# Weight units stored as they stand on chip, tokens stored transposed, norm scales moved behind the projections: a streaming-encoder block on one Trainium2 core

## The chip, the cores and the metric

The kernel runs on one core of one Trainium2 chip. The core has a matrix engine (PE, with PEld for its weight loads), a vector engine (DVE), a scalar engine (ACT), a general engine (POOL) and a queue engine (SP) that issues most transfers; 16 DMA engines move data between the main memory and the on-chip memory. Matmuls write to banks of PSUM, a small memory of which each bank holds 128 x 512 float32 numbers. The metric is device time of one execution in microseconds (us), as the median over runs. The arrays that the kernel is given may be laid out in any way on the host, without arithmetic; that is not part of the time.

## What is computed

All numbers are float32; there are 2048 tokens of 1024 channels.

```python
def reference(x, norm_mix_g, w_in, f_bias, sg_ln_g, sg_w, sg_b, w_out, norm_ffn_g, w_up, w_conv, b_conv, w_down, norm_final_g):
    h = rms_norm(x, norm_mix_g)                  # x * rsqrt(mean(x*x) + eps) * g
    z = h @ w_in                                 # 1024 -> 512 u, 512 v, 512 q, 512 k, 512 values, 8 forget logits
    u, v = gelu(z[:, :512]), gelu(z[:, 512:1024])
    out_a = spatial_gating(u, v, sg_ln_g, sg_w, sg_b)   # u * (masked sg_w @ layernorm(v) + sg_b), blocks of 128 tokens
    c = cumsum(log_sigmoid(f_logit + f_bias))    # per head, over the tokens
    out_b = softmax(q @ k.T / 8 + c[t] - c[s], s <= t) @ values   # 8 heads of 64
    x = x + concat(out_a, out_b) @ w_out
    a = causal_conv3(rms_norm(x, norm_ffn_g) @ w_up, w_conv) + b_conv   # 1024 -> 2 x 2816
    x = x + (silu(a[:, :2816]) * a[:, 2816:]) @ w_down
    return rms_norm(x, norm_final_g)
```

## The kernel before

Each float32 matmul is made of three matmuls in a faster format: both operands are split into a high part and a low part (what the rounding of the high part leaves), and high x high, high x low and low x high are summed in one PSUM bank (`mm3`, L202). So every operand goes through a copy that rounds (on ACT or POOL) and a subtraction on DVE.

The work runs in stages. Stage A (`phase_a`) handles the tokens in two halves of 1024, each of two half-blocks of 512. It normalizes the tokens, turns them so that channels lie on the partitions, splits them, and projects them to keys, queries, values, the two gate inputs u and v, and the forget logits. In the first half the order is keys, queries, values, gates; in the second it is gates, values, queries after keys. From the gates of the first half on, the attention (`b_stream`) is woven in between: `tick` counts matmuls, and each time the count passes a rate (`RATES`) one more step of the attention is issued. Stage C (`c_half`) multiplies by `w_out`, stage D (`d_half`) by `w_up` for the first half; for the second half of the tokens `late_half` does both, and `down` multiplies by `w_down` for all. In the last two, seven products replace eight.

What the change touches, in the kernel before:

- **Weights.** `load_unit` (L151) loads a unit of 128 x 1024 numbers by one DMA on SP (`raw`), casts it to the high part on POOL (L149) and subtracts on DVE (L161). A narrow unit is 128 columns of `w_in` or `w_up` for all eight groups of 128 channels: each row of the matrix that it reads gives 512 B, so a unit is 1024 pieces of 512 B. A wide unit (values and gates, `w_out`) is two groups by 512 columns, 256 pieces of 2 KB. In `late_half`, `up_raw` (L1143) loads narrow units of `w_up` by itself.
- **Tokens.** `a_rows` (L347) loads rows of x (128 tokens x 1024), squares and sums them on ACT (L358), forms the scale on DVE and POOL (L361, L362, a power of -0.5), and in the first half multiplies the rows by it on DVE (L366). `a_norm` (L369) then turns each 128 x 128 piece by PE with an identity matrix (L182, four to a bank), and `split` copies the bank to the high part on ACT with the norm's weight g as a scale (L191) and forms the low part on DVE (L192). For the second half the rows are loaded a second time as [128 tokens, 4, 256 channels], scaled on POOL (L399), and turned in the same way, behind counts of matmuls (`defer`).
- **Small columns.** The per-channel vectors (norm weights, gate bias, convolution) are loaded as rows by seven DMAs (`columns`) and turned by two transposes (`columns_turn`, L266).
- **Gate weights.** `a_gate_w` loads `sg_w`, zeroes the masked part on POOL and turns eight matrices on PE.
- **Projections.** `channels` computes a block of 128 key or query channels by 512 tokens in a bank, copies the high part on ACT (L416), subtracts on DVE (L417) and writes both to memory by four DMAs. `token_major` does values and gates with tokens on the partitions.
- **Constants.** `a_consts` and `b_consts` (masks, a triangle, ones) are filled on POOL behind the first scales.

The order of the instructions on each engine is made by a planner, from priorities and modelled costs: the code gives data flow, priorities (`high_priority`), and a few forced orders (`issue_after`, which queues a block's instructions behind one instruction on the same engine). Rings of buffers have the sizes in `BUFS`; a load into a ring waits until the last reader of the old content is done. The banks `mm` are two.

Of the kernel before, what the change touches and what calls it, by code (L numbers as in the profile page):

```python
# [8 lines left out]
F32 = mybir.dt.float32  # L9
# [23 lines left out]
AHEAD_B, AHEAD_W = 100, 2000  # L33
LAG = 2
# [45 lines left out]
class Block:  # L80
# [70 lines left out]
    def load_unit(self, src, inner):  # L151
# [6 lines left out]
        self.raw_ins = self.dma(v(raw), src).ins  # L158
# [56 lines left out]
    def constants(self):  # L215
# [6 lines left out]
        self.colA = cp.tile([P, 112], F32, name="colA")  # L222
        self.colB = cp.tile([P, 88], F32, name="colB")
# [15 lines left out]
    def columns(self):  # L239

        nc, a = self.nc, self.a
        r0 = self.til(self.sp, [P, TB], F32, "st")[:112, :P]
        r1 = self.til(self.sp, [P, TB], F32, "st")[:88, :P]
        cv = a["w_conv"][0].rearrange("w (c p) -> w c p", p=P)
        self.dma(r0[0:8, :], a["norm_mix_g"][0].rearrange("(c p) -> c p", p=P))
        self.dma(r0[8:16, :], a["norm_ffn_g"][0].rearrange("(c p) -> c p", p=P))
        self.dma(r0[16:24, :], a["sg_b"][0])
        self.dma(r0[24:68, :], cv[0])
        self.dma(r0[68:112, :], cv[1])
        self.dma(r1[0:44, :], cv[2])  # L250
        self.dma(r1[44:88, :], a["b_conv"][0].rearrange("(c p) -> c p", p=P))
        self.rows_c = r0, r1
        self.g_mix = self.colA[:, 0:8]
        self.g_ffn = self.colA[:, 8:16]
        self.sgb = self.colA[:, 16:24]
        self.cw0 = self.colA[:, 24:68]
        self.cw1 = self.colA[:, 68:112]
        self.cw2 = self.colB[:, 0:44]
        self.cb = self.colB[:, 44:88]

    def columns_turn(self):
        nc = self.nc
        r0, r1 = self.rows_c
        for r, n, col in ((r0, 112, self.colA), (r1, 88, self.colB)):
            ps = self.til(self.ap, [P, TB], F32, "tp")
            nc.tensor.transpose(ps[:, :n], r, self.ident[:n, :n])  # L266
            nc.vector.tensor_copy(col, ps[:, :n])

        for t in (self.colA[:, 46:68], self.colA[:, 90:112], self.colB[:, 22:44], self.colB[:, 66:88]):
            nc.vector.tensor_scalar(t, t, 0.5, None, ALU.mult)  # L270


    def phase_a(self):
        tc = self.tc
        with ExitStack() as es:
# [9 lines left out]
            for c in range(2):  # L285
                with tc.issue_after(self.lo_ins[2 + 3 * c]):
                    self.first.append(self.a_unit("k", c))
# [1191 lines left out]
```

## Time and profile before

| | |
|---|---|
| median of 3 runs | 2469.13 us (2466.55 to 2471.33) |
| the profiled execution | 2466.4 us |
| its span, first to last instruction | 2464.6 us |
| busy: PE / DVE / ACT / POOL | 2420.7 / 1740.5 / 1341.4 / 332.0 us |
| moved by DMA | 396.33 MB, 161 GB/s on average |
| PE clock granted, mean | 0.999 of full speed |

The profile page gives busy times and a picture of the span; a trace behind it can be asked for groups of instructions by line, for single instructions in order of time (the timeline), for who waited for whom (the waits), for busy times in chosen stretches (the windows), for one tile's instructions, and for the chain of waits that ends with the last instruction. In such rows `tp<-ident,x` names the tile written and the tiles read, `x46` is a count, and what stands behind the last bar is the engine's idle time before these instructions with what it waited for. A PE row's duration is that of one matmul from entering to leaving; matmuls follow each other before that, so the spacing of their starts is the cost and not the duration.

### The profile page before, as it was taken

What the parts mean: (1) busy time and instruction counts of PE and PEld (TensorE: products, weight loads), DVE (VectorE), ACT (ScalarE), POOL (GpSimd) and SP (SyncE); (2) the same over time, 40 slices, a digit from 0 to 9 for tenths busy, and PEclk for the clock granted to TensorE, in tenths of its full rate; (3) what the DMA queues carried; (4) which work ended last, traced back from release to release, by engine and by line L of the source; (5) the groups of instructions that cost most, each with busy time, mean ns of one, the idle gap of its engine ahead of it and who ended that gap; (6) DMA issues with size and microseconds to landing.
All of it is one profiled execution on the core that took longest, in us unless ns stands there. A gap on an engine that the chain in (4) does not pass through costs nothing.

```text
span 2464.6 us, 32929 instructions
## 1 busy us (share of the span) xinstructions
PE 2420.7 (98%) x11082; PEld 1989.8 (81%) x11082; DVE 1740.5 (71%) x3060; ACT 1341.4 (54%) x2629; POOL 332.0 (13%) x335
## 2 busy tenths in 40 slices
PE   7999999999999999999999999999999999999998
PEld 5788878878878778788888878878888887888887
DVE  6237677565556777878878775488888887957775
ACT  4226676554355555767677673365555555444443
POOL 3214222010113311112111011100000000001000
PEclk9999999999999999999999999999999999999999
DMA  7863544767856544555555445412222329538633
GB/s 209 243 163 105 175 119 135 187 185 208 274 178 205 182 148 157 170 161 181 163 163 181 154 153 205 158 54 93 77 77 88 92 70 319 166 100 289 210 115 121
DMA packets 346244, 396.33 MB, mean 161 GB/s; under 512 B 52924, under 2 KB 222084, under 8 KB 344652
## 3 DMA queue, kind: packets, MB, share of 16 engines
q1 hardware_dynamic: 341036, 370.11, 48.8%
q0 software_dynamic: 5040, 24.12, 2.5%
q8 instruction: 88, 1.44, 0.3%
q14 instruction: 80, 0.66, 0.1%
HBM read 300.56 MB, written 93.72 MB: 160 GB/s over the span
## 4 chain that ended last, share of the span: by engine, by line
PE 88%; DMA 4%; DVE 3%; ACT 2%; issue 1%; POOL 1%; SPq 0%; POOLq 0%; DVEq 0%; ACTq 0%
PE D L1335 16%; PE mm L211 13%; PE mm L209 13%; PE mm L207 13%; PE A L1132 3%; PE A L1134 3%; PE A L1133 3%; PE o L774 2%; PE o L773 2%; PE s L786 2%; PE s L785 2%; PE s L725 2%; PE s L724 2%; PE B L1133 2%; PE B L1134 2%; PE B L1132 2%
## 5 line engine op out<-in xcount | busy, mean ns | idle before, releaser
L207 PE MATMUL mm<-thi,whi 128*128 128x512 f32 x960 | 377.4, 393 | 2.6 <-DVE vn L417 2.0
L209 PE MATMUL mm<-tlo,whi 128*128 128x512 f32 x960 | 377.5, 393 | 0.0
L211 PE MATMUL mm<-thi,wlo 128*128 128x512 f32 x960 | 376.4, 392 | 0.1
L207 PE MATMUL mm<-whi,thi 128*128 128x512 f32 x640 | 253.2, 396 | 1.1 <-DMA thi<-mixh 1.0
L211 PE MATMUL mm<-whi,tlo 128*128 128x512 f32 x640 | 251.1, 394 | 0.8 <-DMA tlo<-mixl 0.8
L209 PE MATMUL mm<-wlo,thi 128*128 128x512 f32 x640 | 250.8, 392 | 0.2 <-DVE wlo L161 0.2
L149 POOL TENSOR_SCALAR whi<-raw 128x1024 fp32r<-128x1024 f32 x108 | 126.5, 1172 | 908.4 <-PE mm L209 551.6
L733 ACT ACTIVATE s<-s,part 128x512 f32<-128x512 f32 (+3 forms) x257 | 150.8, 587 | 151.2 <-DVE part L728 85.4
L207 PEld LDWEIGHTS mm<-thi,whi 128*128 128x128 f32 x960 | 180.4, 188 | 41.8 <-DVE vn L417 2.3
L211 PEld LDWEIGHTS mm<-thi,wlo 128*128 128x128 f32 x960 | 180.5, 188 | 37.9 <-DVE wlo L161 0.6
L209 PEld LDWEIGHTS mm<-tlo,whi 128*128 128x128 f32 x960 | 180.5, 188 | 37.3
L797 DVE TENSOR_TENSOR pl<-e,ph 128x512 fp32r<-128x512 f32 (+2 forms) x212 | 136.7, 652 | 64.1 <-ACT ph L796 31.8
L161 DVE TENSOR_TENSOR wlo<-raw,whi 128x1024 fp32r<-128x1024 f32 x108 | 143.7, 1331 | 50.0 <-POOL whi L149 44.3
L791 ACT ACTIVATE e<-s 128x512 f32<-128x512 f32 (+2 forms) x227 | 116.1, 529 | 83.3 <-DVE s L789 41.6
L1335 PE MATMUL D<-wl,xh 128*128 128x512 f32 x368 | 141.5, 389 | 0.0
L1335 PE MATMUL D<-wh,xh 128*128 128x512 f32 x368 | 140.8, 389 | 0.2 <-DVE xo L1413 0.2
L207 PEld LDWEIGHTS mm<-whi,thi 128*128 128x128 f32 x640 | 120.6, 188 | 24.9 <-DMA thi<-mixh 1.4
L211 PEld LDWEIGHTS mm<-whi,tlo 128*128 128x128 f32 x640 | 120.3, 188 | 24.9 <-DMA tlo<-mixl 1.3
L209 PEld LDWEIGHTS mm<-wlo,thi 128*128 128x128 f32 x640 | 120.6, 188 | 23.2 <-DVE wlo L161 0.4
L1335 PE MATMUL D<-wh,xl 128*128 128x512 f32 x368 | 137.3, 389 | 0.0
L796 ACT ACTIVATE ph<-e 128x512 fp32r<-128x512 f32 (+2 forms) x212 | 117.2, 563 | 36.4 <-PE o L773 29.1
L728 DVE TENSOR_REDUCE part<-s 128x1 f32<-128x512 f32 x144 | 94.8, 683 | 28.3 <-PE s L725 27.6
(1885 smaller groups left out, 5786.3 us busy)
## 6 DMA issues: line engine op xcount, KB each, us to landing
raw<-in_w_up_dram SPq DMA_DIRECT2D x72, 512.0 KB
m<-kx SPq DMA_DIRECT2D x133, 256.0 KB
m<-kx SPq DMA_DIRECT2D x160, 136.0 KB
x<-act SPq DMA_DIRECT2D x84, 256.0 KB
raw<-in_w_in_dram SPq DMA_DIRECT2D x40, 512.0 KB
v<-vd SPq DMA_DIRECT2D x66, 256.0 KB
x<-in_x_dram SPq DMA_DIRECT2D x24, 512.0 KB
raw<-in_w_out_dram SPq DMA_DIRECT2D x24, 512.0 KB
```

What stands on the lines that cost most here:

```text
L149: self.cast_ins = self.nc.gpsimd.tensor_scalar(out, in_, 1.0, 0.0, ALU.mult, ALU.add).ins
L161: nc.vector.tensor_tensor(lo, raw, f32(hi), op=ALU.subtract)
L207: mm(ps, lhsT=ah[k], rhs=bh[k], start=k == 0, stop=False)
L209: mm(ps, lhsT=ah[k], rhs=bl[k], start=False, stop=False)
L211: self.last_mm = mm(ps, lhsT=al[k], rhs=bh[k], start=False, stop=k == n - 1).ins
L733: nc.scalar.activation(ps[:, :n], ps[:, :n], AF.Exp, scale=-1.0, bias=dst, accum_out=ls[:, tt, sb:sb + 1])
L796: nc.scalar.activation(ph[:, c], e[:, c], AF.Copy)
L797: nc.vector.tensor_tensor(pl[:, c], e[:, c], f32(ph[:, c]), op=ALU.subtract)
L1132: mm(ps, lhsT=xh[:, ks], rhs=yh[:, k, :], start=fresh and k == 0, stop=False, **kw)
L1133: mm(ps, lhsT=xh[:, ks], rhs=yl[:, k, :], start=False, stop=False, **kw)
L1134: mm(ps, lhsT=xl[:, ks], rhs=yh[:, k, :], start=False, stop=k == 3, **kw)
L1335: nc.tensor.matmul(bank[t], lhsT=x[i][:, ts], rhs=w[k], start=fresh and j == 0 and i + k == 0, stop=last and i == 1, **kw)
```

## The change

The host hands over other arrays: `w_in`, `w_out` and `w_up` cut into units, each [128, 1024] with 4 KB per partition, in the order that stands on chip; x transposed (`xT`, [1024, 2048]) beside x; the gate weights transposed; the forget weights and all small columns as [128, n]. `w_down` stays. On chip:

- every unit is one DMA with rows of 4 KB; the small columns are one DMA;
- tokens come transposed and are only split, with g as a scale; the row scale is not applied to them. x itself is still loaded for the sums of squares (in the first half as an additional load);
- the row scale is applied behind the projection. Values, u and v have tokens on the partitions: it is the scale operand of the copy that stood there before. Keys and queries have tokens along the row: `a_scales` spreads the scales with four transposes and a copy into a [128, 512] tile `rb`, and DVE multiplies the bank by it into a new tile before the split. Forget logits are multiplied on DVE;
- the start (`a_start`) issues 24 transposes of the identity into a spare bank, loads two key units in quarters between the token chunks, and `first_keys` runs the first half's keys in chunk order over six banks, borrowing four of attention's;
- constants are filled behind the scales of the second half-block.

The diff, cut to its core:

```diff
@@ load_unit
-        self.raw_ins = self.dma(v(raw), src).ins
+        self.raw_ins = self.dma(raw, src).ins
@@ columns
-        self.dma(r0[0:8, :], a["norm_mix_g"][0].rearrange("(c p) -> c p", p=P))
...
+        self.dma(self.cols, a["cols"])
@@ a_start (new)
+        raws = [self.til(self.rawp, [P, 1024], F32, "raw") for _ in range(2)] + [self.til(sp, [P, 1024], F32, "vn") for _ in range(2)]
+        parts = [[self.til(self.wpool, [P, KC, P], F32R, tag) for tag in ("whi", "wlo")] for _ in range(4)]
+        def unit(u, ks):
+            raw = v(raws[u])[:, ks, :]
+            self.dma(raw, v(self.a["w_in"][4 + u])[:, ks, :])
+            hi, lo = [t[:, ks, :] for t in parts[u]]
+            self.cast(hi, raw)
+            nc.vector.tensor_tensor(lo, raw, f32(hi), op=ALU.subtract)
+        junk = self.til(self.ap, [P, TB], F32, "tp")
+        for i in range(WARM):
+            nc.tensor.transpose(junk[:, i % 4 * P:(i % 4 + 1) * P], self.ident, self.ident)
+        self.hT[0] = self.parts(0)
+        xs = [self.til(sp, [P, 2, TB], F32, "x") for _ in range(4)]
+        for k in range(KC):
+            if k % 2 == 0:
+                unit(0, slice(k, k + 2))
+            self.dma(xs[k // 2][:, k % 2, :], self.a["xT"][k * P:(k + 1) * P, 0:TB])
+            self.a_split(0, k, xs[k // 2][:, k % 2, :])
+            if k % 2 == 0:
+                unit(1, slice(k, k + 2))
+        for u in (2, 3):
+            unit(u, slice(0, KC))
...
+        self.a_tokens(0, 1, None, 0)
+        self.scales[0] = [self.a_rows(0, b) for b in range(2)]
+        self.columns_half()
+        with self.tc.issue_after(self.pow_ins):
+            self.a_consts(sp, self.ap)
+            self.b_consts()
@@ a_gate_w
+        self.dma(self.sw, self.a["sgT"].rearrange("s (h t) -> s h t", h=8))
+        self.nc.gpsimd.memset(self.sw[64:128, :, 0:64], 0.0)
@@ a_scales, a_split, a_tokens (new, for a_norm)
+        w = self.til(sp, [P, 4, P], F32, "st")
+        nc.scalar.activation(w, self.scales[half][b].unsqueeze(2).broadcast_to([P, 4, P]), AF.Copy)
+        ps = self.transpose4(self.ap, "tp", [w[:, i, :] for i in range(4)])
+        nc.scalar.activation(self.rb[:, b, :], ps, AF.Copy)
...
+        self.nc.scalar.activation(hi[:, k, :], x, AF.Copy, scale=self.g_mix[:, k:k + 1])
+        self.nc.vector.scalar_tensor_tensor(lo[:, k, :], x, self.g_mix[:, k:k + 1], f32(hi[:, k, :]),
+                                            op0=ALU.mult, op1=ALU.subtract)
...
+        xv = self.a["xT"][:, t0:t0 + TB].rearrange("(q i p) t -> q p i t", i=2, p=P)
+        for q in range(4):
+            x = self.til(self.sp, [P, 2, TB], F32, "x")
+            self.dma(x, xv[q])
...
@@ channels
-            nc.scalar.activation(hi, ps, AF.Copy, scale=sc)
-            nc.vector.scalar_tensor_tensor(lo, ps, sc, f32(hi), op0=ALU.mult, op1=ALU.subtract)
+            t = self.til(sp, [P, TB], F32, "st")
+            nc.vector.scalar_tensor_tensor(t, ps, -0.125 if kind == "q" else 1.0, self.rb[:, b, :], op0=ALU.mult, op1=ALU.mult)
+            self.split_sb(t, hi, lo)
@@ first_keys (new)
+            banks = [self.til(pp, [P, TB], F32, "mm") for _ in range(2)] + [self.scores([P, TB]) for _ in range(3)]
+            banks.append(self.til(self.bpp, [P, TB], F32, "o"))
...
+            for k in range(KC):
+                for u in (0, 1):
+                    mms(u, 0, k)
+            for u, b in ((2, 0), (3, 0)):
+                for k in range(KC):
+                    mms(u, b, k)
+            self.a_forget(half, 0)
+            for u in range(2):
+                for k in range(KC):
+                    mms(u, 1, k)
+                self.a_scales(0, u)
+                for c in (range(2), range(2, 4))[u]:
+                    channels("k", c, None, None, 0, banks[c])
...
@@ values (and u, v alike)
-                nc.scalar.activation(hi, pv, AF.Copy)
-                nc.vector.tensor_tensor(lo, pv, f32(hi), op=ALU.subtract)
+                r = self.scales[half][t // 4][:, t % 4:t % 4 + 1]
+                nc.scalar.activation(hi, pv, AF.Copy, scale=r)
+                nc.vector.scalar_tensor_tensor(lo, pv, r, f32(hi), op0=ALU.mult, op1=ALU.subtract)
@@ a_forget
+            nc.vector.tensor_tensor(z, z, self.scales[half][b].unsqueeze(2).broadcast_to([P, 4, 8]), op=ALU.mult)
@@ c_half, c_late (d_half and up_raw alike)
-                    us = [self.load_unit(w_out[:, 2 * j:2 * j + 2, cs], 512) for j in range(4)]
+                    us = [self.load_unit(self.a["w_out"][4 * col + j], 512) for j in range(4)]
@@ _laid_out (new, on the host)
+    tall = lambda w: w.reshape(KC, P, -1, P).transpose(2, 1, 0, 3).reshape(-1, P, 1024)
+    wide = lambda w: w.reshape(4, 2, P, -1, TB).transpose(3, 0, 2, 1, 4).reshape(-1, P, 1024)
+    w = a["w_in"][0]
+    return dict(w_in=c(np.concatenate([tall(w[:, 1024:2048]), wide(w[:, 0:1024]), wide(w[:, 2048:2560])])),
+                w_out=c(wide(a["w_out"][0])), w_up=c(tall(a["w_up"][0])), xT=c(a["x"][0].T), ...
```

More of the change, by code (lines that the diff above doesn't have):

```diff
@@ L33 @@
 AHEAD_B, AHEAD_W = 100, 2000
+WARM = 24
 LAG = 2
@@ L367, in a_rows @@
[L367 to L392 removed]
+        nc.vector.tensor_scalar(rs, ss, 1.0 / D, EPS, ALU.mult, ALU.add)
@@ L404, in a_half @@
+            self.dma(x, xv[q])
+            for i in range(2):
+                k = 2 * q + i
+                fn = lambda b=b, k=k, x=x, i=i: self.a_split(b, k, x[:, i, :])
+                if wait is None:
+                    fn()
+                else:
+                    self.defer(wait + k * gap, fn)
     def a_half(self, half):
```

229 lines of the change are left out of this document (89 added, 140 removed).

## The prediction

> **What bounds the kernel now.** I read the page first, then the windows of the first 700 us, then who PE waited for, then the groups, the timeline and the chain of the first 100 us, since most of the edit lies there.
>
> ```profile
> span 2464.6 us, 32929 instructions
> ## 1 busy us (share of the span) xinstructions
> PE 2420.7 (98%) x11082; PEld 1989.8 (81%) x11082; DVE 1740.5 (71%) x3060; ACT 1341.4 (54%) x2629; POOL 332.0 (13%) x335
> ```
>
> PE stands still for 2464.6 - 2420.7 = 43.9 us in all. The windows show where:
>
> ```profile
> 0.00:13.80 13.80, 5.57 (x34) 4.88 (x34) 4.99 (x18) 7.34 (x12) 3.04 (x12) 1.00 0.67 204
> 13.80:25.00 11.20, 10.02 (x41) 5.81 (x42) 8.28 (x16) 8.73 (x16) 4.91 (x6) 1.00 1.06 342
> 25.00:50.00 25.00, 21.58 (x114) 15.25 (x115) 17.93 (x31) 8.54 (x15) 13.28 (x22) 1.00 0.50 135
> 50.00:100.00 50.00, 48.04 (x217) 38.76 (x216) 16.57 (x33) 19.75 (x35) 13.20 (x19) 1.00 0.87 272
> ```
>
> The columns are the stretch, its length, the busy time and count of PE, PEld, DVE, ACT and POOL, the clock, the DMA share and GB/s. Up to 100 us PE is busy for 5.57 + 10.02 + 21.58 + 48.04 = 85.2 us, so 14.8 us idle; the other 29 us are strewn over 2365 us. Busy time overstates PE there, because matmuls overlap. The pace of a full PE comes from the chain of waits, a long run of 512-column matmuls, and from a run of 128-column transposes (start, us, what, count):
>
> ```profile
> 2156.20 208.36 PE D L1335 x918
> ```
>
> ```profile
> 305.81 0.89 PE tp L504 x8
> ```
>
> That is 208.36 / 918 = 0.227 us for each 512-column matmul and 0.11 us for each transpose. Since PE is full, what is taken off PE or off the lead-in reaches the end one for one, unless a wait takes its place. So I count the lead-in by useful work: time passed less the work both kernels must do.
>
> ```profile
> L207 PE MATMUL mm<-thi,whi 128*128 128x512 f32 x92 | 36.7, 399 | 2.6 <-DVE vn L417 2.0 <-POOL whi L149 0.6
> L209 PE MATMUL mm<-tlo,whi 128*128 128x512 f32 x92 | 36.2, 393 | 0.0
> L211 PE MATMUL mm<-thi,wlo 128*128 128x512 f32 x91 | 35.7, 392 | 0.1
> L182 PE MATMUL tp<-ident,x 128*128 128x128 f32 x46 | 8.0, 276 | 2.9 <-DVE tlo L192 2.3 <-DVE x L366 0.6
> L568 PE MATMUL mm<-tlo,wf 128*16 128x512 f32 x16 | 6.7, 421 | 0.0
> L566 PE MATMUL mm<-thi,wf 128*16 128x512 f32 x16 | 6.3, 396 | 1.6 <-DVE tlo L192 0.8 <-ACT thi L191 0.8
> ```
>
> These are PE's groups of the first 100 us. The long ones are 92 + 92 + 91 + 16 + 16 = 307, worth 307 x 0.227 = 69.7 us; the forget logits' cumulative sums and small turns, in rows further down, add about 3 us (estimate from their columns at the same pace). So at 100 us the kernel has done 72.7 us of useful work: it is 27.3 us behind a PE that had worked from time 0.
>
> **The change part by part.**
>
> *Lead-in.* The old one in the timeline:
>
> ```profile
> 0.80 1.81 SPq L99 DMA_DIRECT2D x<-in_x_dram  x4
> ...
> 1.19 0.29 POOL masks.py:199 TENSOR_SCALAR_AFFINE_SELECT ident<-ident 128x128 f32<-128x128 f32 x1
> ...
> 4.61 1.06 ACT L358 ACTIVATE ln<-x 128x1024 bf16<-128x1024 f32 x1 [2.54 <-DMA x<-in_x_dram]
> ```
>
> and on PE:
>
> ```profile
> 7.49 0.69 PE L182 MATMUL mm<-ident,x 128*128 128x128 f32 x2 [7.49 <-DVE rstd L361]
> ...
> 9.46 0.85 PE L182 MATMUL s<-ident,x 128*128 128x128 f32 x3
> ...
> 12.25 0.49 PE L182 MATMUL s<-ident,x 128*128 128x128 f32 x3
> ...
> 13.87 0.40 PE L566 MATMUL mm<-thi,wf 128*16 128x512 f32 x1 [0.80 <-DVE tlo L192]
> ```
>
> Load, square, power, scale, transpose, copy and split stand in a row ahead of the first useful matmul at 13.87 us. The change sends transposed tokens straight into the split. The pieces it needs first are the columns (102 KB), a quarter of unit 0 (131 KB) and the first token chunk (262 KB): 0.50 MB, about the 0.52 MB of the old first load, which was there at 4.6 us, but as three issues at 0.45 us each (1.81 / 4). I put it at 5.0 us. Prices of the steps, all from tile views (min/median/max ns):
>
> ```profile
> L971 ACT ACTIVATE xh<-x x74: 615/632/637, 2038.2 to 2442.3; 128x512 fp32r<-128x512 f32 x74
> ...
> L399 POOL TENSOR_SCALAR x<-x,rstd x32: 476/482/1277, 88.4 to 316.0; 128x256 f32<-128x256 f32 x32
> ```
>
> ```profile
> L192 DVE SCALAR_TENSOR_TENSOR tlo<-tp,colA,thi x26: 719/744/753, 20.0 to 350.8; 128x512 fp32r<-128x512 f32 x26
> ```
>
> The high part needs 0.63 us on ACT, the weight cast beside it 0.48 us on POOL: data for a first matmul at 5.6 us. But 24 warm-up transposes stand ahead of it on PE. They wait for the identity (ready at 1.19 + 0.29 = 1.48 us). A row of three (two spacings and the length of the last) lasts 0.85 us at 9.46 and 0.49 us at 12.25, so the second row has the 0.11 us spacing from above; for a slow one I take twice that, 0.21 us (2 x 0.21 + 0.43 = 0.85). The clock opened some 3 us after the first transpose. With 16 slow and 8 fast ones, 16 x 0.21 + 8 x 0.11 = 4.3 us from 1.6 us: they end at 5.9 us. I take 6.0 us for the first useful matmul.
>
> Feeding: each chunk carries 6 matmuls, 1.36 us of PE, against 0.39 MB of DMA, 0.63 us of ACT, 0.48 of POOL, and 0.74 of DVE plus about 0.3 for a quarter of a weight split (estimate from the 1.23 us of a whole one in the fence below). At 342 GB/s a chunk takes 1.15 us and costs nothing; at 204 GB/s 1.93 us, so 8 x 0.57 = 4.6 us lost. I take 1.5 us, between the two. The token and weight splits that follow need no PE or PSUM, so I put other stalls at 1 us (bounds 0 and 5; PE idled 25 - 21.58 = 3.4 us between 25 and 50 us, much of it behind this piece of the chain of waits):
>
> ```profile
> 30.60 1.07 POOL whi L149
> 31.69 1.23 DVE wlo L161
> ```
>
> There a weight cast came out of POOL only behind the constants (masks, ones, zeros), and the splits on DVE and the transposes on PE behind that. Now four units' casts come first and the constants behind the last row scales, ahead only of the query weights, which PE wants only after all the keys. The norm itself moves behind the projection: 8 row loads and squares for the first half now run beside matmuls (8 x 1.06 us of ACT, by the row at 4.61 us), and 8 transposes with copies turn their scales (8 x 0.11 = 0.9 us of PE). They are waited for; see the rivals. New lag: 6.0 + 1.5 + 1 + 0.9 = 9.4 us against 27.3, a **gain of 17.9 us** (bounds 13 to 20).
>
> *Transposes later on.* The 70 transposes of x before 100 us are in the lag. From 100 to 400 us:
>
> ```profile
> L182 PE MATMUL tp<-ident,x 128*128 128x128 f32 x66 | 11.7, 282 | 0.0
> ```
>
> Those 66 (second half of the tokens, and the gate weights that now come turned) go: 66 x 0.11 = 7.3 us; 8 scale transposes come: 0.9 us. **Gain 6.4 us.** The column turns at L266 lie in the lag.
>
> *Other engines.* POOL loses 32 scalings of 0.48 us (15 us). Every key and query block gains one DVE product of about 0.74 us from PSUM, 32 of them, 24 us on an engine with 724 us free; PSUM is let go after that one product instead of after ACT and DVE. ACT's and DVE's split then reads SBUF. Value, gate and forget scales ride on instructions that exist (but 4 small DVE products). Nothing of this is on the path while PE has its two banks; without that cover each late bank costs PE its wait. SP issues 12 token loads and 6 unit loads more (quarters of two units) and 6 column loads less, all ahead of 30 us and at 0.45 us each: 5 us of issuing, spread over the feeding above. I take zero, bounds -4 and +4, since the order of all queues is planned anew.
>
> *4 KB rows.* The same bytes in fewer packets, for all weight units:
>
> ```profile
> q1 hardware_dynamic: 341036, 370.11, 48.8%
> q0 software_dynamic: 5040, 24.12, 2.5%
> ```
>
> Packets, MB, share of 16 engines. q1 moves 1085 B a packet in 0.488 x 2464.6 x 16 / 341036 = 56 ns, 19 B/ns; q0's 4786 B packets take 196 ns, 24 B/ns. So long rows are about a fifth cheaper. PE, however, hardly waits on weights. Its longest waits (us in total, times, longest):
>
> ```profile
> PE mm L182 <- DVE rstd L361: 7.5, 1, 7.5
> PE o L774 <- DVE pl L797: 3.5, 4, 1.7
> ```
>
> The first is the lead-in, the next attention's own split; in the groups of the first 100 us, where units are few, a weight cast (POOL whi) held PE for 0.6 us. I take nothing for it. [...]
>
> **Sum.** 17.9 + 6.4 = 24.3 us. The profiled execution took 2466.4 us (1.8 around its span), so it would be 2442.1; the median of the runs is 2469.1 (2466.6 to 2471.3), from which I count: **2444.8 us**.
>
> **The rivals.**
>
> *The scales come late.* The first key banks wait for the row scales, which lie behind 8.1 MB of transfers (columns, 3.1 MB of chunks and units, 1 MB of units, two times 2.1 MB). PE gets there at about 6 + 1.5 + 96 x 0.227 + 16 x 0.227 + 24 x 0.227 = 38 us. At 272 GB/s the rows are there at 32 us and the scale 3 us later; at 204 GB/s at 42 and 45 us, and the second half-block's, with 10.2 MB, at 55 us, when PE wants them at 38 + 7 + 5.5 = 50. Price 7 + 5 = 12 us: 2457 us. For it: 204 GB/s is what the first stretch ran at; against: the start-up latency is in that figure, and 342 was reached right behind it.
>
> *Waits further on shrink too.* POOL and the transfers are relieved where attention begins. If half of the 29 us of idle PE after 100 us goes, 2430 us. Against: the waits above are on attention's own loads and on DVE, which gets more work.
>
> *Cold start.* If transposes don't open the clock, the first 3 us of real matmuls run at half pace and the 24 transposes take 24 x 0.21 = 5.0 us: 1.5 + 0.7 = 2.2 us, 2447 us. The rows at 9.46 and 12.25 us speak against it, since only transposes had run by then. [...]
>
> *Slower: the new DVE product holds the banks.* In the second half's keys and queries, beside attention, each of 16 blocks waits on DVE before its bank is free. PE needs 24 x 0.227 = 5.4 us a block, and two banks turn, so it decides only where DVE is over 5.4 us late, and ends slower than before from 24.3 / 16 = 1.5 us beyond that, on every block.
>
> ```profile
> 500.00:600.00 100.00, 100.00 (x473) 79.00 (x472) 56.92 (x132) 51.06 (x115) 6.69 (x6) 1.00 0.66 182
> ```
>
> DVE is 57% busy there and 16 x 0.74 us over 150 us adds 8%. At 2 us beyond, 32 us are lost: 2477 us. Only bursts speak for it.
>
> **How the numbers follow.** Forecast 0.60 (own range 2438 to 2453: bounds of lead-in and planning), scales late 0.14, waits shrink 0.13, cold start 0.05, slower 0.05, the turned gain given back elsewhere to within 0.2% of no change (some 5 us, what a measurement here can tell) 0.03. Cutting the slower case and the tails, the range is 2432 to 2459. Faster: 0.91; same: 0.04; slower: 0.05.
>
> **What would show it.** First useful matmul near 6 us; no L182 transposes of x; useful work at 100 us over 88 us; 8 fewer us of PE between 100 and 400 us; PE's waits from 400 us on as before. I am wrong if PE idles between 30 and 60 us on the scales' product, if transfers of token chunks starve PE before 17 us, or if the stretch behind 400 us moves by over 5 us either way.

## The result, and the profile after

| | before | after |
|---|---|---|
| median of 4 runs each | 2467.84 us (2464.51 to 2471.33) | 2444.48 us (2439.76 to 2446.41) |
| the profiled execution, its span | 2466.4, 2464.6 us | 2445.03, 2443.3 us |

The kernel became faster by 23.4 us; the ratio is 0.9902, with a 95% interval of 0.9882 to 0.9923. The forecast was 2444.8 us. The total came out as worked out, but not all of its terms did: two amounts that were not in the sum, a gain and a loss, are nearly as large as the lead-in itself.

The head of the page of the kernel after:

```profile
span 2443.3 us, 32802 instructions
## 1 busy us (share of the span) xinstructions
PE 2415.5 (99%) x10984; PEld 1984.8 (81%) x10984; DVE 1750.7 (72%) x3086; ACT 1347.4 (55%) x2635; POOL 317.4 (13%) x303
```

PE now stands still for 2443.3 - 2415.5 = 27.8 us, 16.1 less than before. Its busy time fell by only 5.2 us, though 98 instructions went; a part of the span, 13.7 us from 675.0 us and 3.4 us from 760.4 us, is spent at half the clock. The windows of the kernel after, in the same columns (stretch, length, busy time and count of PE, PEld, DVE, ACT, POOL, clock, DMA share, GB/s):

```profile
0.00:13.80 13.80, 11.45 (x51) 9.80 (x52) 6.84 (x16) 5.88 (x8) 4.89 (x15) 1.00 0.83 247
13.80:25.00 11.20, 11.20 (x51) 9.16 (x50) 9.88 (x15) 5.16 (x8) 3.68 (x3) 1.00 0.97 363
25.00:50.00 25.00, 23.68 (x111) 17.73 (x110) 9.30 (x19) 16.24 (x30) 11.56 (x20) 1.00 0.84 310
50.00:100.00 50.00, 50.00 (x229) 38.81 (x228) 29.19 (x54) 20.59 (x35) 8.14 (x9) 1.00 0.79 217
300.00:400.00 100.00, 99.85 (x505) 83.91 (x504) 70.42 (x134) 67.47 (x125) 32.47 (x18) 1.00 0.40 118
600.00:700.00 100.00, 94.17 (x412) 74.61 (x411) 53.20 (x105) 50.75 (x115) 13.06 (x16) 0.93 0.62 198
800.00:1000.00 200.00, 200.00 (x910) 165.31 (x909) 156.84 (x312) 124.29 (x271) 41.05 (x38) 1.00 0.52 167
```

and three of the kernel before that the prediction did not show:

```profile
300.00:400.00 100.00, 94.67 (x476) 78.35 (x476) 80.25 (x145) 69.67 (x133) 36.91 (x26) 0.98 0.45 132
600.00:700.00 100.00, 99.21 (x456) 82.10 (x454) 50.35 (x97) 41.78 (x98) 17.82 (x20) 1.00 0.83 276
800.00:1000.00 200.00, 195.02 (x879) 160.04 (x878) 152.06 (x296) 114.94 (x250) 44.20 (x40) 1.00 0.52 166
```

The idle time of the first 100 us went from 14.8 to 3.7 us. Between 300 and 400 us PE gained 5 us. But between 600 and 700 us the kernel after is the worse one: PE idles 5.8 us instead of 0.8 and the granted clock is 0.93.

To add this up I use the prediction's measure over the whole span: the *lag*, time passed less the useful matmuls begun by then, each at the pace of a full PE (0.227 us for 512 columns, 0.172 for 384, 0.115 for 256, 0.11 for 128; turns of x, identity, scales and columns count nothing). The useful work is 2375.5 us in every kernel here. At 25 us, for instance, the kernel after has begun 100 matmuls, 24 of them warm-up: 76 x 0.227 = 17.3 us, so the lag is 7.7 us. Worked out so from the matmul records of the traces (us):

```
time                   25   100 |  200   400   600 |  700   800 | 1600  2430
before               15.9  27.3 | 28.0  48.7  51.1 | 52.9  56.7 | 75.1  80.3
after                 7.7  10.8 | 12.9  16.3  20.1 | 35.1  41.5 | 53.9  59.2
second_half_old       8.2  11.2 | 12.0  22.4  25.2 | 34.0  35.4 | 48.7  54.5
first_half_old       15.9  29.7 | 31.8  36.1  39.7 | 49.6  65.0 | 74.0  81.5
early_fill            8.9  12.1 | 13.8  21.0  25.3 | 36.2  37.9 | 51.6  54.5
early_fill_ahead      7.5  10.9 | 19.1  25.7  30.5 | 34.0  37.2 | 51.6  55.4
```

(The last four are experiments, told below.) The kernel after gains 27.3 - 10.8 = 16.5 us up to 100 us; then (51.1 - 27.3) - (20.1 - 10.8) = 14.5 us up to 600 us; it loses (41.5 - 20.1) - (56.7 - 51.1) = 15.8 us between 600 and 800 us; and gains 5.9 us behind that. The sum is 21.1 us, the difference of the two profiled spans within 0.2 us.

**The place of the loss.** PE's share of each stretch around it, after:

```profile
655.00:664.00 9.00, 9.00 (x48) 7.37 (x47) 4.89 (x11) 5.15 (x10) 0.00 (x0) 1.00 0.53 174
664.00:675.00 11.00, 8.04 (x47) 5.65 (x45) 8.76 (x16) 7.92 (x18) 0.00 (x0) 1.00 0.48 136
675.00:690.00 15.00, 13.05 (x32) 8.96 (x33) 8.23 (x24) 9.81 (x26) 0.00 (x0) 0.54 0.52 175
690.00:700.00 10.00, 10.00 (x46) 8.17 (x45) 4.27 (x8) 5.24 (x9) 0.00 (x0) 1.00 0.19 52
```

First PE is full, then 73% busy for 11 us, then at 0.54 of the clock for 15 us, then full again. PE's timeline in that hole has only the attention's own steps and the turns of the first C block's rows. Several of the steps wait for another engine's part of the step before, or for a load (in brackets, idle time and what ended it):

```profile
667.84 0.70 PE L745 MATMUL s<-m,t 128*128 128x512 f32 x2 [1.01 <-DMA t<-qx]
...
673.62 0.50 PE L744 MATMUL s<-m,t 96*128 96x512 f32 x1 [0.51 <-ACT s L753]
...
675.09 0.79 PE L744 MATMUL s<-m,t 96*128 96x512 f32 x1 [0.73 <-DVE op L837]
```

At this seam two interleaved streams join. The second block of stage C multiplies the attention's result for the second half-block, so it can't begin before the last write of that result (`mixh<-ph`); the other stream, projections and the first block of C, has by then run out. The additions of stage C (in the tile view of `acc`, from first to last) and that last write, before:

```profile
L861 DVE TENSOR_TENSOR acc<-mm,acc x16: 680/691/693, 641.6 to 754.7; 128x512 f32<-128x512 f32 x16
```

```profile
691.34 0.32 SPq L99 DMA_DIRECT2D mixh<-ph  x1
```

and after:

```profile
L880 DVE TENSOR_TENSOR acc<-mm,acc x16: 680/691/692, 604.0 to 738.0; 128x512 f32<-128x512 f32 x16
```

```profile
675.85 0.33 SPq L100 DMA_DIRECT2D mixh<-ph  x1
```

Stage C starts 37.6 us earlier, the attention's half is done only 15.5 us earlier. The distance between the two grew from 49.7 to 71.9 us.

Not all of the 15.8 us lies here. Within 20 us of the attention's last write the lag grows by 13.0 us in the kernel after and by 2.6 us before: 10.4 us. Some 4 us more are lost behind that, mostly between 740 and 770 us, where the clock drops once more (3.4 us at half clock from 760.4 us), and the rest ahead of it. These smaller losses are not followed up here.

### The profile page after: what moved, and what is told of

Read it like the earlier page. It is cut to its first block, busy times and chain, and to the rows that moved or that the text cites. A ratio compares the mean times of both kernels' runs of the same rounds, so it can differ in the third digit from the quotient of the medians.

```text
span 2443.3 us, 32802 instructions
## 1 busy us (share of the span) xinstructions
PE 2415.5 (99%) x10984; PEld 1984.8 (81%) x10984; DVE 1750.7 (72%) x3086; ACT 1347.4 (55%) x2635; POOL 317.4 (13%) x303
## 4 chain that ended last, share of the span: by engine, by line
PE 88%; DMA 5%; DVE 3%; issue 1%; ACT 1%; SPq 1%; POOL 0%; DVEq 0%; POOLq 0%; ACTq 0%
PE mm L208 13%; PE mm L210 13%; PE mm L212 13%; PE D L1350 13%; PE A L1148 3%; PE A L1150 3%; PE A L1149 3%; PE o L794 2%; PE o L793 2%; PE s L745 2%; PE s L744 2%; PE s L806 2%; PE s L805 2%; PE B L1149 2%; PE B L1150 2%; PE B L1148 2%
## 5 line engine op out<-in xcount | busy, mean ns | idle before, releaser
L208 PE MATMUL mm<-thi,whi 128*128 128x512 f32 x912 | 358.3, 393 | 0.9 <-DVE st L395 0.9
L210 PE MATMUL mm<-tlo,whi 128*128 128x512 f32 x912 | 358.7, 393 | 0.0
L212 PE MATMUL mm<-thi,wlo 128*128 128x512 f32 x912 | 358.0, 393 | 0.0
L150 POOL TENSOR_SCALAR whi<-raw 128x1024 fp32r<-128x1024 f32 (+1 forms) x112 | 126.1, 1127 | 1021.6 <-PE mm L210 541.1
L208 PEld LDWEIGHTS mm<-thi,whi 128*128 128x128 f32 x912 | 171.7, 188 | 36.6 <-DVE st L395 1.3
L210 PEld LDWEIGHTS mm<-tlo,whi 128*128 128x128 f32 x912 | 171.8, 188 | 35.2
L212 PEld LDWEIGHTS mm<-thi,wlo 128*128 128x128 f32 x912 | 171.8, 188 | 34.8
L162 DVE TENSOR_TENSOR wlo<-raw,whi 128x1024 fp32r<-128x1024 f32 x104 | 134.0, 1289 | 58.8 <-POOL whi L150 58.2
L811 ACT ACTIVATE e<-s 128x512 f32<-128x512 f32 (+2 forms) x216 | 110.4, 528 | 81.4 <-DVE s L809 39.2
```

What stands on the lines that cost most here:

```text
L150: self.cast_ins = self.nc.gpsimd.tensor_scalar(out, in_, 1.0, 0.0, ALU.mult, ALU.add).ins
L162: nc.vector.tensor_tensor(lo, raw, f32(hi), op=ALU.subtract)
L208: mm(ps, lhsT=ah[k], rhs=bh[k], start=k == 0, stop=False)
L210: mm(ps, lhsT=ah[k], rhs=bl[k], start=False, stop=False)
L212: self.last_mm = mm(ps, lhsT=al[k], rhs=bh[k], start=False, stop=k == n - 1).ins
```

## The experiments

The theory, from the two traces: the lead-in carries the gain; turns and scaling of the second half are worth little, because what is won there is handed back at the seam. Rivals: the long rows do it; the later transposes do it; the hole is due to the attention's rate or to its own chain of waits. Ratios are to the kernel before in runs beside them; its median was 2465.4 to 2469.0 us in the different series, so a few us between medians of two series tell little.

### What carries the gain

**The second half of the tokens as before** (all else as after): its rows scaled on POOL, turned on PE, no product behind keys and queries.

```diff
-                    self.a_tokens(1, t // 4, 14 if t == 3 else 16, 9 if t == 3 else 6)
+                    self.o_norm(1, t // 4, self.rows1[t // 4], 14 if t == 3 else 16, 9 if t == 3 else 6)
...
-                    self.scales[1] = [self.a_rows(1, b) for b in range(2)]
+                    self.rows1 = [self.a_rows(1, b) for b in range(2)]
+                    self.scales[1] = [ones, ones]
```

> The changed kernel with the second half of the tokens taken as in the kernel before (scaled on POOL, turned on PE, split from the bank, no scale behind the projections); first half, columns, gate weights and units as changed. It is the counterpart of the first half taken the old way, which gave back all of the gain. If the two halves are worth something each and the order decides (doubled transposes cost 6.2 us), 2449 to 2453 us. If only the lead-in reaches the end, 2442 to 2447 us.

Measured: 2438.73 us, ratio 0.9886 (0.9869 to 0.9902), below both expectations. The first half's new path, together with the units, columns and gate weights, brings 28.6 us: all of the gain and perhaps 5 us more than the whole change (0.9902, 0.9882 to 0.9923; the intervals overlap, so "more" is not shown). In the lag table it is 5.1 us behind the kernel after at 600 us, a little less than the 6.4 us of the transposes, and loses 10.2 us between 600 and 800 us instead of 21.4. PE's longest wait there is the join itself, the second block of stage C on the attention's result (us in total, times, longest):

```profile
PE mm L208 <- DMA thi<-mixh: 4.6, 1, 4.6
```

**The first half of the tokens as before** (second half, columns, gate weights and units as after).

```diff
-            self.a_start()
+            rows = self.o_rows(0, 0, True)
+            self.o_norm(0, 0, rows, None, 0)
...
+            self.o_norm(0, 1, self.o_rows(0, 1, True), 16, 6)
```

> The changed kernel with the first half of the tokens taken as in the kernel before (rows loaded, normalized, turned on PE, two key units first, no warm-up, no scale behind the projections); second half, columns, gate weights and units as changed. My theory: the lead-in's 18 to 20 us are given back, the second half's transposes stay away: 2461 to 2464 us. Rival (the gain is mostly in the second half and in what becomes free there): 2452 us or less.

Measured: 2467.56 us, ratio 1.0002 (0.9989 to 1.0016), above the 2461 to 2464 us of the theory. The second half's new path, with the units, columns and gate weights, brings nothing. It does win at first: 11.4 us by 600 us (51.1 against 39.7 in the table). Between 600 and 800 us all of it goes: the lag grows by 25.3 us, where that of before grows by 5.6. Its windows:

```profile
600.00:700.00 100.00, 94.84 (x437) 76.11 (x436) 58.05 (x115) 49.06 (x116) 15.22 (x18) 0.99 0.74 236
700.00:800.00 100.00, 93.71 (x405) 74.97 (x405) 59.48 (x111) 50.67 (x108) 26.69 (x25) 0.93 0.56 186
```

These show the same picture as the hole of the kernel after: 5 to 6 us idle in each stretch, and the clock down behind it. Of the 25.3 us, 11.9 lie within 20 us of the attention's last write and 10.6 behind that.

**The turns put back as useless work:** 64 transposes of the second half's tokens into a spare bank, beside the splits of the kernel after.

```diff
-                fn = lambda b=b, k=k, x=x, i=i: self.a_split(b, k, x[:, i, :])
+                fn = lambda b=b, k=k, x=x, i=i: (half and self.transpose4(self.ap, "tp", [x[:, i, c * P:(c + 1) * P] for c in range(4)]), self.a_split(b, k, x[:, i, :]))
```

> The changed kernel with 64 transposes of the second half's tokens put back on PE, into a spare bank that nobody reads; the split does not wait for them. My theory (every transpose on a full PE reaches the end): 64 x 0.11 = 7.0 us more, 2451.5 us. Rival (they fitted into waits): 2444.5 us.

Measured: 2450.68 us, 0.9930 (0.9916 to 0.9943), 6.2 us above the kernel after, though the intervals overlap. In its trace the lag is some 9 us larger at 600 us and 4 us larger at the end. The price of 0.11 us for each turn on a full PE, 64 x 0.11 = 7.0 us, fits but is not pinned down by this. That taking the real ones away still brings nothing is no contradiction: there, the loss between 600 and 800 us is larger by 11.2 us (21.4 against 10.2).

**Only the units** of 4 KB rows, in the kernel before, and the reverse, **only the units undone** in the kernel after:

```diff
-        self.raw_ins = self.dma(v(raw), src).ins
+        self.raw_ins = self.dma(raw, src).ins
```

> The kernel before with only the weight units handed over as 4 KB rows; tokens, norms and columns as before. My theory (PE is full, weights are not waited for): no change, 2468 us, within 5 us either way because the order of the queues is planned anew. Rival (shorter transfers carry much of the gain): half of the 23 us or more, 2456 us or less.

> The changed kernel with the weight units read from the matrices as they were, in rows of 512 B and 2 KB; all else as changed. My theory: the gain stays, 2444 us, within 5 us; the first useful matmul is later by under 1 us. Rival (4 KB rows carry the gain): 2456 us or more.

Measured: 2466.02 us, 0.9988 (0.9979 to 0.9997), and 2444.85 us, 0.9907 (0.9893 to 0.9921), within 0.4 us of the kernel after. The units gain some 3 us in the first pair (0.7 to 5.2 by the interval), and nothing to be seen in the second. Nor are the long rows a fifth cheaper. The queue of the units-only kernel (packets, MB, share of 16 engines) moves the same bytes as that of before in 99,328 fewer packets:

```profile
q1 hardware_dynamic: 241708, 370.11, 47.3%
```

47.3 against 48.8% of 16 engines is 3% less transfer time, but for the whole queue, of which the units are a part. By the packets they are 104 narrow and 48 wide units (104 x 896 + 48 x 128 = 99,328 packets less), 152 x 0.524 = 79.7 of the 370 MB. The time of all the queue's packets, summed, fell from 19,230 to 18,671 us in the first pair and from 19,185 to 18,948 us in the second. Against the 4140 us that 79.7 MB cost at the old queue's mean of 19.2 B/ns, the units became 13% and 6% cheaper (an estimate; the two pairs differ by as much as that). The prediction had inferred the fifth from a comparison of two queues that do different things.

**No warm-up:** `WARM = 24` set to 0 in the kernel after.

> The changed kernel without the 24 warm-up transposes. My theory (transposes open the clock): the first useful matmul comes at the same time as with them, 7.3 us, since it waits for the token split; the granted clock opens only 3 us or so after that, so the first 12 to 14 matmuls are 0.43 us apart and the useful work at 25 us is 2 to 3 us less. [...]

Measured in a single run: 2446.75 us, beside a median of 2468.97 for the kernel before. That can't tell 2 us, but PE's timeline can. After:

```profile
1.53 5.00 PE L286 MATMUL tp<-ident 128*128 128x128 f32 x24 [1.53 <-POOL ident masks.py:199]
7.35 0.70 PE L422 MATMUL mm<-thi,whi 128*128 128x512 f32 x2 [0.82 <-ACT thi L362]
8.05 0.50 PE L423 MATMUL mm<-tlo,whi 128*128 128x512 f32 x1
```

and without warm-up:

```profile
7.41 1.19 PE L422 MATMUL mm<-thi,whi 128*128 128x512 f32 x2 [7.41 <-ACT thi L362]
8.40 0.63 PE L423 MATMUL mm<-tlo,whi 128*128 128x512 f32 x1
8.83 0.63 PE L424 MATMUL mm<-thi,wlo 128*128 128x512 f32 x1
```

The first useful matmul comes at the same time. Without warm-up the starts are 0.43 us apart, half pace, up to 11.6 us; with it the clock is open before the first one, from 6.0 us on. At 25 us the lag is 9.3 instead of 7.7 us: the warm-up is worth 1.6 us in this pair, where 2 to 3 were expected. (In the eight other traces with the same warm-up the clock opened between 4.3 and 7.5 us, and the lag at 25 us was 7.5 to 8.9 us.) With warm-up the 24 transposes alone opened the clock: at 6.0 us nothing else had run on PE, and their starts go from 0.21 us apart to 0.11.

**No product behind the second half's keys and queries:** ACT and DVE split from the bank as before. The kernel leaves the row scale of these blocks out, with the turns that spread it.

```diff
-            t = self.til(sp, [P, TB], F32, "st")
-            nc.vector.scalar_tensor_tensor(t, ps, -0.125 if kind == "q" else 1.0, self.rb[:, b, :], op0=ALU.mult, op1=ALU.mult)
-            self.split_sb(t, hi, lo)
+            if half:
+                nc.scalar.activation(hi, ps, AF.Copy, scale=sc)
+                nc.vector.scalar_tensor_tensor(lo, ps, sc, f32(hi), op0=ALU.mult, op1=ALU.subtract)
```

> The changed kernel without the row scale on keys and queries of the second half (this part of the computation is left out; the split reads the bank as in the kernel before): 16 DVE products and 8 transposes fewer. My theory (the product is covered by the two banks): 2443.5 us, within 4 us. Rival (the product holds the banks and shifts what is behind it): 2436 us or less.

Measured: 2438.80 us, 0.9878 (0.9863 to 0.9894), 5.7 us below the kernel after, with overlapping intervals. It fits neither expectation and stays inconclusive. The lag at 600 us is the same (20.6 against 20.1), so the product delays nothing where it stands, and the hole stands as well (15.4 us of lag from 600 to 700 us, 15.0 after). The difference appears behind 700 us: the drop of the clock at 760 us is missing (the granted clock is 1.00 from 700 to 800 us). Why was not looked into.

### What makes the hole at the seam

**The rate of the attention:** a step is issued every 3.6 instead of every 4.0 matmuls of the second half.

```diff
-RATES = [3.5, 4.0, 4.4, 3.6]
+RATES = [3.5, 3.6, 4.4, 3.6]
```

> The changed kernel with attention woven in a step per 3.6 instead of 4.0 matmuls in the second half of stage A. Theory of the seam: the changed kernel loses 13 us between 600 and 700 us since attention is less far ahead when the second block of stage C waits for it, so PE thins out there and its clock falls to half; with more attention done before, 8 to 12 us come back: 2433 to 2437 us, and the clock is not at half there. Rival (the loss is an accident of the planned order and turns up elsewhere): 2440 to 2449 us.

Measured: 2444.02 us, 0.9897 (0.9883 to 0.9910): no difference to the kernel after. The attention's last write is at 674.4 instead of 675.9 us, and the hole is there. The rate moved the attention by 1.5 us only, so it isn't the rate that holds it back.

**The attention's own chain:** `LAG`, the steps by which its second product trails its scores, 1 instead of 2.

> The changed kernel with attention's products one block behind its scores instead of two (LAG 1, the same arithmetic), so that its chain of waits is worse covered. If attention's own pace makes the hole between 655 and 690 us, its first 16 pieces end later than 680 us, PE loses over 15 us between 600 and 700 us and the time is 2450 us or more. If the hole comes from the loads and weights of stage C, 2442 to 2448 us.

Measured: 2446.28 us, 0.9918 (0.9901 to 0.9935), last write at 674.5 us. With a step less to cover them, the waits inside the chain should have hurt if they set the pace of the attention as a whole. It shows no sign of that. (Inside the hole, where nothing else is left, PE does wait on them: in the kernel after 0.51 us for ACT's part and 0.73 us for DVE's, by the rows above.)

**The attention begun earlier:** its steps are issued from the third value block of the first half on, and not from the gates on, in the kernel after and, as a control, in the kernel before.

```diff
@@ values
+                if half == 0 and t == 2:
+                    self.start_fill(self.b_stream([(h, tb) for tb in range(4) for h in range(8)]), RATES[0])
@@ a_half
-            self.start_fill(self.b_stream([(h, tb) for tb in range(4) for h in range(8)]), RATES[0])
```

> The changed kernel with attention's first step issued behind the third block of values instead of behind the eighth, 5 x 24 matmuls or 27 us earlier in the program. The rate did not move the seam, so the theory now is that attention's pace is set by its own chain of waits: it gained 15 us of lead and the projections 36 us, and the difference is paid where the second block of stage C needs attention's result. If so, attention ends its first 16 pieces 10 to 25 us earlier, the hole between 655 and 690 us shrinks to under 4 us and the time falls by 6 to 12 us, to 2433 to 2439 us. Rival (the hole is made by the loads and weights of stage C itself): attention earlier, the hole as it is, 2442 to 2447 us.

> The kernel before with the same earlier start of attention: a control. There the seam costs only some 2 us, so by the theory of attention's pace 2463 to 2468 us (0 to 4 us less); if the earlier start is worth the same by itself in both kernels, 2456 to 2461 us.

Measured: 2436.32 us, 0.9865 (0.9847 to 0.9882), and 2468.34 us, 0.9999 (0.9989 to 1.0008). The first has the lowest median of this study, 8.2 us below the kernel after; its interval just touches the kernel after's. In the kernel before the same edit moves the attention's last write from 691.3 to 663.9 us and wins nothing: the join costs only 2.6 us there to begin with. In the kernel after the time came as expected, and the hole shrank to under 4 us, but by another road: the first pair of heads is out 23 us earlier (172.6 instead of 195.4 us), the last write only 3.4 us earlier:

```profile
672.41 0.38 SPq L100 DMA_DIRECT2D mixh<-ph  x1
```

What moved is the other stream: stage C now starts at 620.8 us instead of 604.0, with more of the attention woven in ahead of it. The distance is 51.6 us, and PE's row for the place of the hole, which in the kernel after holds 30.1 us of work, is:

```profile
655.00:690.00 35.00, 33.07 (x158) 27.34 (x157) 18.05 (x32) 17.00 (x39) 4.11 (x7) 0.95 0.65 199
```

Part of the gain is lost again ahead of stage C: at 604.6 us PE waits 3.5 us for a load of queries (`t<-qx`), and the clock is at half from 606.8 to 613.6 us (over 600 to 625 us PE is busy for 21.47 us and the granted clock is 0.86).

**Priority:** as the last kernel, and the attention's instructions rank higher with the planner.

```diff
-AHEAD_B, AHEAD_W = 100, 2000
+AHEAD_B, AHEAD_W = 400, 2000
```

> The early start of attention together with a higher priority of its steps in the planner (400 places ahead instead of 100). If the planner's order still holds attention back, its first 16 pieces end 5 to 15 us before the 672 us of the early start alone and the time falls by 3 to 6 us more, to 2431 to 2433 us; if its pace is that of its chain of waits, nothing changes: 2435 to 2438 us.

Measured: 2440.92 us, 0.9895 (0.9880 to 0.9910). The hole is gone. Last write and the stretch of the hole:

```profile
655.99 0.34 SPq L100 DMA_DIRECT2D mixh<-ph  x1
```

```profile
120.00:140.00 20.00, 17.58 (x70) 13.33 (x69) 8.55 (x21) 4.75 (x13) 2.09 (x2) 0.91 0.78 217
...
655.00:690.00 35.00, 35.00 (x164) 28.62 (x162) 18.22 (x38) 21.51 (x47) 7.43 (x12) 1.00 0.70 231
```

PE is busy for all 35 us at full clock. It fits neither expectation, though. The first row shows the price: projections that now rank lower make PE wait at 120 to 140 us, with a drop of the clock, and the lag at 200 us is 19.1 instead of 13.8 us. In total it is no better than the kernel that it was made from. So the planner's order decides when the attention is done, and with the attention done in time there is no hole; but closing it by rank costs as much elsewhere.

All kernels together, from the same rows of each (us): first addition of stage C, last write of the attention's half, their distance; by how much that write comes behind the eighth and last addition of C's first block; lag added within 20 us of the write, and from 600 to 800 us.

```
                   C begins  attention done  distance  behind block 1  at the join  600 to 800
before_early_fill     644.2           663.9      19.7           -28.0          0.3         6.1
early_fill_ahead      624.7           656.0      31.3           -16.4          0.4         6.7
before                641.6           691.3      49.7             2.4          2.6         5.6
units_only            639.9           690.5      50.6             2.5          1.4         4.1
early_fill            620.8           672.4      51.6             6.1          3.9        12.6
second_half_old       615.3           669.0      53.7             9.1          8.4        10.2
first_half_old        626.0           695.8      69.8            25.4         11.9        25.3
units_undone          605.5           675.6      70.1            25.0         11.6        22.6
turns_doubled         613.6           684.4      70.8            24.8         13.7        20.4
rate_36               603.1           674.4      71.3            25.6         11.9        19.7
lag_1                 603.2           674.5      71.3            25.7         13.1        22.7
after                 604.0           675.9      71.9            26.0         13.0        21.4
no_product            602.2           675.8      73.6            25.3         13.7        18.0
no_warm               605.4           682.1      76.7            26.0         12.7        24.1
```

Where the attention is done before C's first block or at most 2.5 us behind it, the join costs 0.3 to 2.6 us; at 6.1 us it costs 3.9, at 9.1 us 8.4, and from 24.8 us on 11.6 to 13.7. What the last column has beyond that lies ahead of the join or behind it, and differs from kernel to kernel. The cost sets in where the first stream runs out: behind the first addition its block of C has 7 more, of 24 matmuls each, 7 x 24 x 0.227 = 38.1 us, with attention's steps between them. A kernel that speeds the projections up without the attention pays here.

## Why the prediction was right, and where it was not

- **The lead-in, 17.9 us (bounds 13 to 20):** measured 16.5 us at 100 us. Without the first half's path, to which it belongs, the rest of the change is worth nothing (1.0002); with it and without the second half's path all of the gain is there (0.9886). Its terms: the first useful matmul came at 7.35 us and not 6.0. The first chunk was there at 5.19 us (predicted 5.0), but ACT's first instruction then began with a step that the sum lacks (ACT's timeline, after):

```profile
5.19 1.28 ACT L362 ACT_TABLE_LOAD   x1 [5.19 <-DMA x<-in_xT_dram]
6.49 1.40 ACT L362 ACTIVATE thi<-x,cols 128x512 fp32r<-128x512 f32 x2
```

  In the kernel before this load of ACT's function table ran at 0.79 us, while the first rows were still on their way; in the kernel after it waits with the first split for the chunk. The mis-sized steps cancel in part: feeding cost about nothing and not 1.5 us, since the transfers ran at 363 GB/s from 13.8 to 25 us and PE was busy for all 11.2 us. Behind that the lag grew by 3.1 us up to 100 us; 1.9 were forecast for stalls and scale turns.
- **Warm-up:** 24 transposes were put at 4.3 us (16 slow, 8 fast) and took 5.00; the clock opened at 6.0 us, 4.5 us after the first one, where I said 3. That the transposes alone open it was right here; the worth was some 1.6 us.
- **Later transposes, 6.4 us: this step failed.** The price of one fits (some 6 us for 64 added), and by 600 us they show as 5.1 us of lag. As a part of the change they bring nothing: with the second half's path but not the first half's the ratio is 1.0002, and the kernel without that path (0.9886) is no slower than the whole change (0.9902). The sentence that failed is "what is taken off PE or off the lead-in reaches the end one for one, unless a wait takes its place": here a wait took its place 300 us later.
- **"PE's waits from 400 us on as before", and wrong "if the stretch behind 400 us moves by over 5 us either way": it moved, by 15.8 us for the worse and 5.9 for the better.** By its own test the prediction was wrong here, and the total was right because a gain that it lacked, 8.1 us between 100 and 600 us beyond the transposes' 6.4, and the 5.9 us behind 800 us stand against the loss between 600 and 800 us, with 14.0 against 15.8. That these two nearly cancel is luck. Of the 8.1 us this is the most direct sign, the largest of PE's waits from 100 to 600 us in the kernel before (us in total, times, longest):

```profile
PE s L724 <- DMA m<-kx: 2.5, 1, 2.5
PE o L774 <- DVE pl L797: 2.1, 2, 1.7
PE s L758 <- DVE m L742: 1.9, 1, 1.9
```

  and all that is left of them after:

```profile
PE mm L208 <- DVE st L395: 0.9, 1, 0.9
```

  All waits of these stretches are 6.9 us before and 0.9 after, and the clock of 0.98 in the row of 300 to 400 us is 3.4 us at half clock from 345.1 us, up to 1.7 us, which the kernel after doesn't have: 6.0 + 1.7 = 7.7 of the 8.1 us. This is the rival "waits further on shrink", which came true in its place and was then swallowed between 600 and 800 us. Both half changes show it (the lag grows by 14.0 and 10.0 us from 100 to 600 us, against 23.8 before), so it hangs on neither half alone. The units alone leave it (some 24 us); the columns and gate weights, which both half changes keep, weren't tried alone.
- **Other engines, zero:** on the product's own account PE waited 0.9 us in all (the row above), so the slower rival, banks held by DVE, is out. What the new order of all queues would do was put at ±4 us; that bound was too narrow by far.
- **4 KB rows, zero:** right within some 3 us, though the fifth beside it was too much: 6 to 13% by the two pairs above. In the kernel before, the hardware queue's (`q1`) packets of 512 B ran at 17.6 B/ns on average and those of 4096 B at 23.1, though they carry different arrays.
- **Scales late:** did not come; PE idles 25 - 23.68 = 1.3 us between 25 and 50 us, on the spread of the scales. **Cold start:** refuted by the clock that stood open from 6.0 us on, behind transposes alone.
- **Two readings to put right; neither moves a term by much.** The 0.11 us of a turn was read from `tp L504`, which are 128-column matmuls of the gates and no turns. Turns at full clock do come at the same pace: 8 of them (`dn<-ident,ar`) last 1.03 us in the kernel after, of which the last one alone takes some 0.27 us. And the 8.1 MB ahead of the row scales come to 8.4 MB from their own parts.

What stays open: why the planner places the attention as it does when neither its rate nor its lag matters, and whether an order exists that closes the hole without the loss at 120 us. The kernels from 2436 to 2441 us differ by less than their intervals tell.

## What to carry to other kernels

Work taken off a serial lead-in moves everything behind it along, and here it reached the end; work taken off one of two interleaved streams was here worth something only until they next joined, so before counting it, look for the join and for how much work the faster stream has left when it gets there. A sum that comes out right isn't yet a set of right steps: check the stretches that were forecast not to move. And a transfer's cost per byte should be taken from the same queue with one thing changed, not from two queues that differ in more than the row, and the saving set against the bytes that changed.

## What the hardware did that was not expected

- The granted clock fell to half with no long wait on PE: from 664 to 675 us its longest wait was 1.01 us and it was 73% busy, and that was followed by 13.7 us at half clock (675.0 to 688.7 us). Apart from the span's last microseconds, the kernel after has one more drop, 3.4 us from 760.4 us, and the kernel before a single one, 3.4 us from 345.1 us. In the kernel after they cost up to 8.5 us in all, half of 13.7 and of 3.4 us, against 3.0 us of idle time in the 11 us ahead of the long one.
- Transposes of the identity alone opened the clock, 4.5 us after the first of them; without the warm-up it opened 4.2 us after the first matmul. Over the nine traces with the warm-up it took 2.8 to 6.0 us.
- ACT's first table load, 1.28 us, went from hidden to exposed without a line about it in the diff. ACT's first instruction is now a different one: its wait for the chunk stands as an instruction of its own (5.14 us) ahead of the table load, where in the kernel before the load ran at once and only the squares behind it waited.
